# Linear attention on one core: the tiles that DMAs touch move to multiples of 2 KB in SBUF

## The chip, the cores and the metric

The kernel runs on one core of one Trainium2 chip. A core has TensorE (PE in the profile, with weight loads as PEld), VectorE (DVE), ScalarE (ACT), GpSimd (POOL) and SyncE (SP), a working memory of 128 partitions (SBUF), an accumulator memory (PSUM) and 16 DMA engines between SBUF and HBM. The metric is the device time in microseconds, less being better. The kernel before takes 126.41 us, the median of three runs (126.26 to 126.86).

## The reference

Inputs Q, K and V are float32 of 8 batches x 12 heads x 512 positions x 64 features. The attention is linear: no softmax, but a positive feature map.

```python
Q_feat = np.maximum(0, Q) + 1
K_feat = np.maximum(0, K) + 1
KV = np.einsum('bhkd,bhkv->bhdv', K_feat, V)
K_sum = np.sum(K_feat, axis=2)
numerator = np.einsum('bhqd,bhdv->bhqv', Q_feat, KV)
denominator = np.einsum('bhqd,bhd->bhq', Q_feat, K_sum)
return (numerator / (denominator[:, :, :, None] + 1e-10)).astype(np.float32)
```

In bytes: three inputs of 12.58 MB are read and one output of 12.58 MB is written.

## The kernel before

The 96 heads are taken in six steps (s = 0 to 5), each of 2 x 8 heads. A partition holds 32 consecutive positions of one head, so a step's tile `k_raw`, `v_raw` or `q_raw` is 128 partitions x 2 x 32 x 64 in bfloat16: 8 KB in each partition, 1 MB in all. The DMA that fills it reads float32 (2 MB) and casts on the way; such DMAs are issued by GpSimd (line 128), which also issues the stores of steps 0 to 4 (line 135). SyncE issues the very first K load, uncast, into a buffer of the output pool (line 121), and the three stores of the last step (line 135).

For each step, VectorE makes K features (`kf`, line 144, in two copies, each of which keeps every second head of 16 partitions) and Q features (`qf`, line 164), VectorE and ScalarE copy V blocks into `v_all` (line 156), whose zeros keep the four groups of 32 partitions apart, and TensorE accumulates K^T V and the sums of K together in `kva_ps` (line 175). ScalarE brings these into `kva` (lines 189 and 193). TensorE transposes Q features (line 199), ScalarE copies them to `qt` (line 204), TensorE multiplies them by `kva` (line 216), and VectorE takes the reciprocal of the denominators (line 232) and multiplies it in (line 233) into the output tile `o_sb`: float32, 128 partitions x 8 x 8 x 64, so 16 KB in each partition. A store takes every second of the eight rows of 2 KB of each partition, which land in HBM as rows of 2 KB.

The order of the work is written out by hand for each engine, as lists of tasks (`ORDER`); each engine works through its list in order, and semaphores follow from which tiles are read and written. GpSimd's list is its loads and stores:

```python
    POOL="""
        lv2 lk2 lq2 lv3 lq3 lk3 lk4 lv4 lq4 s00 lv5 lk5 s01 lq5 s10 s11 s20 s21 s30 s31 s40 s41
    """,
```

`lk4` is the K load of step 4, `s21` the second store of step 2. Loads of steps 0 and 1 go ahead of the list. The pools of `k_raw`, `v_raw`, `q_raw`, `kf`, `qf` and `qt` have two buffers each, so a load of step s waits for the last reader of step s - 2; the output pool has four.

A tile's SBUF address follows from the order in which the pools are opened. They are laid one behind the other from byte 16512 of each partition (8 x 2 KB + 128). The constants come first: the identity, masks, both `v_all` of 16640 bytes and both `kva` of 2080 bytes, together 37,888 bytes, so that the pools behind them begin at byte 54,400, which is 26 x 2048 + 1152. The tiles that follow are of 8 KB or 16 KB, so every tile behind the constants, those that DMAs touch among them, begins 1152 bytes beyond a multiple of 2 KB.

Of the kernel before, what the change touches and what calls it, by code (L numbers as in the profile page):

```python
# [8 lines left out]
FP32 = mybir.dt.float32  # L9
# [4 lines left out]
BANK = 512  # L14
OUT_BUFS = 4
KF_BUFS = 2
LOWEST = -3.4028234663852886e38

TASKS = dict(
# [33 lines left out]
def kernel(  # L53
# [13 lines left out]
    P = 128  # L67
# [12 lines left out]
    v_dram = view(V, ROWS)  # L80
    o_dram = view(out, C)

    const = ctx.enter_context(tc.tile_pool(name="const", bufs=1))
    k_pool = ctx.enter_context(tc.tile_pool(name="k_pool", bufs=2))
    v_pool = ctx.enter_context(tc.tile_pool(name="v_pool", bufs=2))
    q_pool = ctx.enter_context(tc.tile_pool(name="q_pool", bufs=2))
    kf_pool = ctx.enter_context(tc.tile_pool(name="kf_pool", bufs=KF_BUFS))
    qf_pool = ctx.enter_context(tc.tile_pool(name="qf_pool", bufs=2))
    mid_pool = ctx.enter_context(tc.tile_pool(name="mid", bufs=2))
    out_pool = ctx.enter_context(tc.tile_pool(name="out_pool", bufs=OUT_BUFS))  # L90
    recip_pool = ctx.enter_context(tc.tile_pool(name="recip", bufs=4))
    psum_kva = ctx.enter_context(tc.tile_pool(name="psum_kva", bufs=2, space=bass.MemoryType.PSUM))
    psum = ctx.enter_context(tc.tile_pool(name="psum", bufs=2, space=bass.MemoryType.PSUM))
    psum_qt = ctx.enter_context(tc.tile_pool(name="psum_qt", bufs=2, space=bass.MemoryType.PSUM))

    identity = const.tile([P, P], BF16, name="identity")
    ones = const.tile([P, 4], BF16, name="ones")
    zero = const.tile([P, 1], FP32, name="zero")
# [143 lines left out]
    def masks():  # L242
# [7 lines left out]
        nc.vector.tensor_scalar(  # L250
            out=shift, in0=least, scalar1=-1.0, scalar2=-LOWEST, op0=ALU.add, op1=ALU.mult
        )
# [14 lines left out]
    def needs(engine, task):  # L267
# [10 lines left out]
        if x == "kf":  # L278
            n = 2 * s + at[0] - KF_BUFS
            return [("load", s, "k"), ("kv", n // 2, n % 2, 3)]  # L280
# [136 lines left out]
```

## Time and profile before

| | us |
|---|---|
| median of three runs | 126.41 |
| the runs | 126.26 to 126.86 |
| the profiled execution | 126.19 |
| its span, first to last instruction | 124.4 |
| VectorE busy | 93.5 (75%) |
| TensorE busy | 82.0 (66%) |
| ScalarE busy | 74.3 (60%) |
| GpSimd busy | 25.1 (20%) |

The page describes one execution. The busy rows cut the span into 40 slices of 3.1 us; a digit is the busy share in tenths, and in the DMA row the mean share of the 16 DMA engines. The GB/s row counts the bytes of a packet as recorded, which for a casting load is the bfloat16 size, half of what is read from HBM. DMA queue q0 is GpSimd's, whose descriptors software writes, q1 is SyncE's, written by hardware, and q8 and q14 fetch instructions. A DMA's work is cut into packets, each on one of 16 DMA engines; at its end each engine writes 4 bytes to say that it is done. The trace records start, duration and size of each packet, and its DMA view counts them for any stretch of time. "us to landing" is from a DMA's issue to the last of these 16 notes.

### The profile page before, as it was taken

The page shows a single profiled execution, that of the slowest core. Times are in us where ns is not written, and L with a number is a line of the kernel's source. Part 1 is how long each engine was busy: PE and PEld are TensorE (multiplying, and loading weights), DVE is VectorE, ACT ScalarE, POOL GpSimd, SP SyncE. Part 2 cuts the span into 40 slices and gives each one's busy share as a digit, 9 for nine tenths or more (in the row PEclk, how much of TensorE's full clock was granted, in tenths as well). Part 3 has the DMA queues.
Part 4 walks back from the last instruction along what each step waited for, and adds up shares of the span by engine and source line. Part 5 has one row for each costly group of instructions (what it writes and reads, how often), then busy time and mean ns, then how long its engine had stood idle before and what let it go on. Part 6 is the DMA issues. An engine that isn't in the chain of part 4 may idle for free.

```text
span 124.4 us, 2353 instructions
## 1 busy us (share of the span) xinstructions
PE 82.0 (66%) x960; PEld 61.8 (50%) x960; DVE 93.5 (75%) x188; ACT 74.3 (60%) x94; POOL 25.1 (20%) x52
## 2 busy tenths in 40 slices
PE   0000099963999895879439998979598798956000
PEld 0000078842767773568326776856376686633000
DVE  4799953459589596995969799999389999699100
ACT  7538000665586999829991289955999936830000
POOL 6991042000006000063000391202200202020000
PEclk9999999998699999999986999999999999995555
DMA  3999999999999999999999999999999999999993
GB/s 84 336 215 212 217 215 216 211 211 221 211 215 217 216 207 219 213 216 213 213 213 216 215 216 291 296 215 215 288 300 238 399 417 417 410 398 398 385 387 138
DMA packets 8731, 32.13 MB, mean 258 GB/s; under 512 B 528, under 2 KB 528, under 8 KB 8592
## 3 DMA queue, kind: packets, MB, share of 16 engines
q0 software_dynamic: 7504, 28.84, 94.4%
q1 hardware_dynamic: 1216, 3.15, 6.9%
q8 instruction: 7, 0.11, 0.3%
q14 instruction: 4, 0.03, 0.1%
HBM read 37.75 MB, written 12.58 MB: 405 GB/s over the span
## 4 chain that ended last, share of the span: by engine, by line
DMA 50%; DVE 20%; ACT 8%; issue 7%; PE 5%; POOL 2%; POOLq 0%
DMA q_raw<-in_Q_dram 35%; DMA k_raw<-in_K_dram 15%; DVE o_sb L233 9%; ACT v_all L156 5%; DVE kf L144 4%; DVE qf L164 4%; ACT qt L204 2%; PE kva_ps L175 2%; DVE v_all L156 2%; DVE recip L232 2%; PE o_ps L216 2%; PE qt_ps L199 1%; ACT kva L189 1%; POOL v_raw L128 1%; POOL k_raw L128 0%
## 5 line engine op out<-in xcount | busy, mean ns | idle before, releaser
L175 PE MATMUL kva_ps<-v_all,kf 128*128 128x260 bf16 x384 | 53.4, 290 | 23.1 <-DVE v_all L156 18.0
L175 PEld LDWEIGHTS <-kf 128*128 128x128 bf16 x384 | 36.7, 102 | 32.8 <-DVE v_all L156 19.2
L156 ACT COPY v_all<-v_raw 32x2048 bf16<-32x2048 bf16 x19 | 36.0, 1896 | 7.7 <-DMA v_raw<-in_V_dram 4.1
L233 DVE TENSOR_TENSOR o_sb<-o_ps,recip 128x512 f32<-128x512 f32 x48 | 33.2, 692 | 1.7
L204 ACT COPY qt<-qt_ps 128x1024 bf16<-128x1024 bf16 x24 | 23.8, 1014 | 10.1 <-PE qt_ps L199 9.8
L216 PE MATMUL o_ps<-kva,qt 128*64 128x130 bf16 x384 | 20.9, 235 | 6.2 <-DVE o_sb L233 4.2
L144 DVE TENSOR_SCALAR kf<-k_raw,shift,least 128x2048 bf16<-128x2048 bf16 x22 | 16.9, 811 | 9.2 <-DMA k_raw<-in_K_dram 7.8
L156 DVE COPY v_all<-v_raw 32x2048 bf16<-32x2048 bf16 x29 | 20.1, 693 | 1.2 <-DMA v_raw<-in_V_dram 0.5
L216 PEld LDWEIGHTS <-qt 128*64 128x64 bf16 x384 | 13.2, 114 | 14.8 <-DVE o_sb L233 6.0
L189 ACT CAST kva<-kva_ps 64x256 bf16<-64x256 f32 x24 | 8.9, 371 | 17.1 <-PE kva_ps L175 16.7
L199 PE MATMUL qt_ps<-identity,qf 128*128 128x128 bf16 x192 | 15.0, 223 | 3.4 <-ACT qt L204 1.9
L199 PEld LDWEIGHTS <-qf 128*128 128x128 bf16 x192 | 12.3, 100 | 4.9 <-issue 2.0
L135 POOL DMA_DIRECT2D out_dram<-o_sb x10 | 8.0, 803 | 30.1 <-DVE recip L232 18.7
L128 POOL DMA_DIRECT2D v_raw<-in_V_dram x7 | 4.8, 683 | 39.6 <-DVE recip L232 17.9
L164 DVE TENSOR_SCALAR qf<-q_raw 128x1024 bf16<-128x1024 bf16 x24 | 8.8, 429 | 5.2 <-DMA q_raw<-in_Q_dram 5.2
L232 DVE RECIPROCAL recip<-o_ps 128x8 f32<-128x8 f32 x48 | 9.6, 200 | 2.4 <-PE o_ps L216 2.1
L128 POOL DMA_DIRECT2D k_raw<-in_K_dram x6 | 4.2, 697 | 13.3 <-DVE kf L144 13.3
L128 POOL DMA_DIRECT2D q_raw<-in_Q_dram x6 | 5.1, 842 | 1.2 <-DVE qf L164 1.2
L258 DVE MEMSET v_all<- 128x2600 f32 x2 | 4.5, 2225 | 1.1 <-issue 1.1
L193 ACT CAST kva<-kva_ps 64x4 bf16<-64x4 f32 x24 | 4.1, 171 | 0.0
L259 ACT COPY v_all<-zero 128x1560 f32<-128x1560 f32 x2 | 2.9, 1488 | 0.0
L144 DVE TENSOR_SCALAR kf<-o_sb,shift,least 128x2048 bf16<-128x2048 f32 x2 | 2.6, 1340 | 0.0
(18 smaller groups left out, 6.6 us busy)
## 6 DMA issues: line engine op xcount, KB each, us to landing
out_dram<-o_sb POOLq DMA_DIRECT2D x10, 1024.0 KB, 22.4
q_raw<-in_Q_dram POOLq DMA_DIRECT2D x6, 1024.0 KB, 23.8
k_raw<-in_K_dram POOLq DMA_DIRECT2D x5, 1024.0 KB, 19.3
v_raw<-in_V_dram POOLq DMA_DIRECT2D x5, 1024.0 KB, 18.3
o_sb<-in_K_dram SPq DMA_DIRECT2D x1, 1024.0 KB, 4.9
v_raw<-in_V_dram POOLq DMA_DIRECT2D x2, 512.0 KB, 8.6
out_dram<-o_sb SPq DMA_DIRECT2D x1, 1024.0 KB, 8.7
out_dram<-o_sb SPq DMA_DIRECT2D x2, 512.0 KB, 7.7
```

Source lines behind the costliest of these rows:

```text
L128: nc.gpsimd.dma_start(out=t[:, ns[0] : ns[-1] + 1], in_=drams[x][:, 2 * s + ns[0] : 2 * s + ns[-1] + 1])
L135: engine.dma_start(out=o_dram[:, 8 * s : 8 * s + 8][:, ms], in_=outs[s][:, ms], single_packet=engine is nc.gpsimd,)
L144: nc.vector.tensor_scalar(out=kf[:, :, a], in0=raw["k", s, n], scalar1=shift[:, a : a + 1], scalar2=least[:, a : a + 1], op0=ALU.add, op1= ...
L156: copy(out=v_alls[n][ps, :, b * D : b * D + D], in_=raw["v", s, n][ps])
L164: nc.vector.tensor_scalar(out=qf[:, :, cs, n], in0=rows[:, :, cs], scalar1=1.0, scalar2=1.0, op0=ALU.add, op1=ALU.max,)
L175: nc.tensor.matmul(kva_pss[s, n], lhsT=kfs[s, n][:, c].rearrange("p a d -> p (a d)"), rhs=v_alls[n][:, c], start=(c == 0), stop=(c == ROWS ...
L189: nc.scalar.copy(out=kva[po, a::2, n, 0:D], in_=kva_ps[pi, 0 : 4 * D].rearrange("p (b d) -> p b d", b=4),)
L199: nc.tensor.transpose(qt_ps[:, c, r], qfs[s][:, r, 2 * i + c], identity)
L204: copy(out=qts[s][:, 2 * i : 2 * i + 2], in_=qt_pss.pop((s, i)).rearrange("p c r q -> p c q r"),)
L216: nc.tensor.matmul(o_ps[64 * t : 64 * t + 64, c // 2, (c % 2) * W : (c % 2) * W + W], lhsT=qts[s][:, 4 * i + c, 16 * k : 16 * k + 16], rhs ...
L232: nc.vector.reciprocal(out=recip, in_=cells[:, :, :, :, D:D1])
L233: nc.vector.tensor_tensor(out=outs[s][:, e + 2 * u :: 4, 4 * i : 4 * i + 4].rearrange("p n (b c) d -> p b c n d", b=2), in0=cells[:, :, :, ...
```

## The change

A pool `head` with one tile of 480 float32 (1920 bytes in each partition) that nothing reads or writes is opened first. It fills the 1920 bytes from 16512 to 18432, which is 9 x 2048. Behind it come the pools of the tiles that DMAs read or write (`k_raw`, `v_raw`, `q_raw`, then the output tiles), then `kf`, `qf`, `qt` and the reciprocals, and last the constants. All tiles of 8 and 16 KB now begin at multiples of 2 KB. The constants' addresses have the same remainders by 2 KB as before. Each engine's instructions, their order and their waits are the same; they carry other addresses.

```diff
+HEAD = 480
...
-    const = ctx.enter_context(tc.tile_pool(name="const", bufs=1))
+    head = ctx.enter_context(tc.tile_pool(name="head", bufs=1))
     k_pool = ctx.enter_context(tc.tile_pool(name="k_pool", bufs=2))
     v_pool = ctx.enter_context(tc.tile_pool(name="v_pool", bufs=2))
     q_pool = ctx.enter_context(tc.tile_pool(name="q_pool", bufs=2))
+    out_pool = ctx.enter_context(tc.tile_pool(name="out_pool", bufs=OUT_BUFS))
     kf_pool = ctx.enter_context(tc.tile_pool(name="kf_pool", bufs=KF_BUFS))
     qf_pool = ctx.enter_context(tc.tile_pool(name="qf_pool", bufs=2))
     mid_pool = ctx.enter_context(tc.tile_pool(name="mid", bufs=2))
-    out_pool = ctx.enter_context(tc.tile_pool(name="out_pool", bufs=OUT_BUFS))
     recip_pool = ctx.enter_context(tc.tile_pool(name="recip", bufs=4))
+    const = ctx.enter_context(tc.tile_pool(name="const", bufs=1))
...
+    head.tile([P, HEAD], FP32, name="spacer")
```

## The prediction

> **What bounds the kernel now.** I read the page first: its rows by slices, the DMA queues, the chain of waits.
>
> ```profile
> span 124.4 us, 2353 instructions
> ...
> DVE  4799953459589596995969799999389999699100
> ...
> DMA  3999999999999999999999999999999999999993
> GB/s 84 336 215 212 217 215 216 211 211 221 211 215 217 216 207 219 213 216 213 213 213 216 215 216 291 296 215 215 288 300 238 399 417 417 410 398 398 385 387 138
> ...
> q0 software_dynamic: 7504, 28.84, 94.4%
> q1 hardware_dynamic: 1216, 3.15, 6.9%
> ...
> DMA 50%; DVE 20%; ACT 8%; issue 7%; PE 5%; POOL 2%; POOLq 0%
> ```
>
> The DMA row is 9 from the second slice to the last but one, and the two data queues together hold 101% of the 16 DMA engines (packets of one engine overlap a little). No compute engine is as full: VectorE has 75% in the page. The chain gives DMA only half, because it steps back from an issue to the compute that released it; whether that compute mattered depends on whether the DMA queue was empty when the issue came. So next, when POOL's issues went out and when they landed: two lines of POOL's timeline, then the issue lines of the DMA view for 53 to 54.5 us and for 109 to 116:
>
> ```profile
> 53.87 0.71 POOL L128 DMA_DIRECT2D k_raw<-in_K_dram  x1 [13.25 <-DVE kf L144]
> ...
> 108.93 0.75 POOL L135 DMA_DIRECT2D out_dram<-o_sb  x1 [3.90 <-DVE recip L232]
> ```
>
> ```profile
> k_raw<-in_K_dram POOLq DMA_DIRECT2D x1, 1024.0 KB, 14.1
> ```
>
> ```profile
> out_dram<-o_sb POOLq DMA_DIRECT2D x1, 1024.0 KB, 9.9
> out_dram<-o_sb SPq DMA_DIRECT2D x1, 1024.0 KB, 8.7
> out_dram<-o_sb SPq DMA_DIRECT2D x2, 512.0 KB, 7.7
> ```
>
> The last number is us from issue to landing. A load's own transfer is 4.9 us (below) and a store's 2.5, so the K load that waited longest for compute still stood some 9 us behind other transfers, the last POOL store 7.4 us, and the two halves on SP about 5 (7.7 less 2.7 for both). The DMA engines never run dry: compute could be some 5 us late anywhere without being seen, and a faster compute engine buys nothing. The kernel's time is the sum of its DMA packets, so I need the price of one packet of each kind. The DMA view of four stretches, 20 to 70 us (loads alone), 98 to 108 (POOL's stores), 109 to 116 (the same, later), 118.6 to 121.6 (SP's stores):
>
> ```profile
> DMA packets 2767, 10.72 MB, mean 214 GB/s; under 512 B 160, under 2 KB 160, under 8 KB 2762
> ...
> q0 software_dynamic: 2762, 10.66, 105.9%
> q8 instruction: 3, 0.05, 0.4%
> q14 instruction: 2, 0.02, 0.1%
> ```
>
> ```profile
> DMA packets 1075, 4.16 MB, mean 416 GB/s; under 512 B 64, under 2 KB 64, under 8 KB 1073
> ...
> q0 software_dynamic: 1073, 4.13, 101.7%
> ```
>
> ```profile
> DMA packets 713, 2.78 MB, mean 397 GB/s; under 512 B 38, under 2 KB 38, under 8 KB 711
> ```
>
> ```profile
> DMA packets 596, 1.16 MB, mean 386 GB/s; under 512 B 30, under 2 KB 30, under 8 KB 596
> ```
>
> Packets under 512 B are the 4-byte completion writes. Loads: (2762 - 160)/16 = 162.6 packets per DMA engine in 50 us, 307.5 ns each, 306 without the 0.5% for instruction fetches. The packet records give it sharper: on the engine that finishes first the completions of whole loads (16 packets per engine) follow at 4.895 us and of half loads (8) at 2.461, so a load packet, 8192 B read and 4096 B written, takes 304.2 ns and a completion 27. POOL's stores: 1009/16 = 63.1 per engine in 10 us, 158.6 ns; on the engine that finishes first whole stores follow at 2.49 us, so (2490 - 27)/16 = 153.9 ns for a packet of 4096 B, two rows of 2 KB. Late POOL stores: 673/16 = 42.1 in 7 us, 166.4. SP's stores, packets of one row of 2 KB: 566/16 = 35.4 in 3 us, 84.8.
>
> These make up the span: the first K load ends at 5.1; 17.5 loads x 4.895 = 85.7; 10 POOL stores x 2.49 = 24.9; 64 SP packets x 84.8 ns = 5.4; sum 121.1. The last packet ends at 123.2. The 2.1 left are instruction fetches of up to 1.1 us on single engines and the slower late stores. The profiled execution's own time is 126.19, 1.8 beyond its span and 0.2 under the median of the three runs, 126.41.
>
> **The change part by part.** It adds a spacer tile that nothing touches, and reorders pools. Engine streams, waits and DMA shapes are the same instruction for instruction; only SBUF addresses differ. Nothing is moved past a queue and no wait is added.
>
> *Compute operands.* kf, qf, qt, recip, v_all and kva lie elsewhere. kf keeps its distance to k_raw in these remainders, qf to q_raw; v_all and kva keep their remainder to 2 KB. No row shows any price for the address of an operand; the bounds are zero and whatever the 5 us of slack swallows, so zero either way. If the cover were gone, the chain's DVE pieces (0.69 us per norm) would be what is late next.
>
> *Load packets*, 280 per DMA engine. Their SBUF side starts 128 B past a multiple of 256 (1152 = 4 x 256 + 128), afterwards on one. They move 4096 B into SBUF but read 8192 from HBM, and whatever the write has extra lies under the read. From above: per byte the load packet (304.2/8192 = 37.1 ps) is cheaper than the store packet (37.6), so no row shows a faster one. A line through both kinds has 2 x 153.9 - 304.2 = 3.6 ns per packet that does not go with bytes; if all of that were alignment, 280 x 3.6 = 1.0 us goes. Taken: zero, since it is the same 3.6 for one row as for two.
>
> *POOL store packets*, 160 per engine: they read two rows of 2 KB from SBUF, each now starting halfway between multiples of 256. Were half a 256 B piece read for nothing at each row, 128 B at 26.9 B/ns = 4.75 ns, a packet would carry 9.5 ns. But it stands only 153.9 - 152.1 = 1.8 above half a load packet, so there is no room for it. Bounds 0 and 160 x 3.6 = 0.6 us gained; taken zero.
>
> [...]
>
> *SP store packets*, 64 per engine: 84.8 ns against 3.6 + 2048 x 0.0367 = 78.8 by the line, 6.0 more. That would fit one half piece (4.75). But the first K load's 8192 B packets on SP's queue are recorded at 309 ns, and the instruction fetches of 8192 B during the run, which do not touch the kernel's tiles, at 309 to 322. So packets issued by hardware look dearer whatever they touch. Bounds: 64 x 6.0 = 0.38 us gained, or nothing; taken nothing.
>
> *A loss.* All DMA tiles sat at one remainder before, so the trace shows no other. The nearest row of a dearer packet is the late stretch, 166.4 less 158.6, 7.8 ns above the same packets earlier. Bounds 0 and, for the some 115 POOL store packets per engine before 109 us, 115 x 7.8 = 0.9 us; taken zero.
>
> Sum: 126.19 + 0 for the profiled execution; between that and the median of the runs I say 126.3.
>
> **The rivals.**
>
> *Boundaries cost after all (faster).* Half a piece on each SBUF row read goes: 160 x 9.5 + 64 x 4.75 = 1.8 us, giving 124.5. For it: the SP packets carry about one such piece. Against: the POOL packets. In part, it can be the SP packets (0.38) and the late stores' 7.8 ns on 45 packets (0.35): 0.73, giving 125.6. Chance of a gain over 0.63 us from here: 0.23.
>
> *Rows at multiples of 2 KB make SBUF accesses collide (slower).* The place is the packet's SBUF side; the cause of the late stretch's dearer packets would reach all stores: +0.9, giving 127.2. It decides from 0.63 us, that is 5.5 ns on each of those 115, or 2.3 on each load packet. For it: that stretch shows that the same packet can get dearer with the loads gone. Against: within a DMA engine all rows stood at one remainder before too, and stores at 98 to 108 us show nothing of it. Chance 0.14.
>
> *The change does not do what it says.* The spacer could be dropped as unused. It is not: the first K tile goes from byte 54400 to 18432, which is 9 x 2048. Chance 0.01, and the time would be 126.3 too.
>
> **How the numbers follow.** No measurable change 0.62 and the idle spacer 0.01; faster 0.23; slower 0.14. A measurement of this kernel tells 0.5%, 0.63 us, from no change. The forecast is 126.3, its own range 125.7 to 126.9. The range of all reaches to 124.8, leaving out the whole boundary gain (0.08), and to 127.2, leaving out loads that collide as well (0.06).
>
> **What would show it.** Right: loads alone again some 163 packets per DMA engine in 50 us, POOL stores 63 in 10 us, SP stores 35 in 3 us, and a full DMA row. The boundary rival shows 67 POOL stores in 10 us and SP packets near 79 ns; the collision shows fewer than 61, or loads under 160. I am wrong if the packets' price moves at all; wrong about the cover if the DMA row gets a gap and packets keep their price.

## The result and the profile after

The changed kernel takes 125.77 us (median of 20 runs, 125.47 to 126.67), the kernel before 126.44 in its 20 runs beside it: the ratio is 0.9952 with a 95% interval of 0.9937 to 0.9966, a gain of 0.61 us (the medians stand 0.67 apart). The forecast was 126.3, with a range of 125.7 to 126.9: no change that a measurement can tell, the limit being put at 0.5%. The measured 0.48% is inside that limit, but the interval excludes no change: the change does something, and the forecast said that it does nothing.

The profiled execution took 125.95 us with a span of 124.2. Its page:

```profile
span 124.2 us, 2353 instructions
...
DVE  4799963459589696995979799999389999799200
...
DMA  3999999999999999999999999999999999999992
GB/s 95 333 214 214 215 212 212 215 214 216 214 215 214 212 214 215 215 215 215 215 212 214 215 215 277 310 199 214 277 318 227 389 414 417 416 414 416 408 406 107
...
q0 software_dynamic: 7504, 28.84, 94.5%
q1 hardware_dynamic: 1216, 3.15, 6.7%
```

The DMA row is full as before, and in the GB/s row the slices of loads are what they were (some 215). The difference stands in the last eight slices: before they fell from 417 to 410, 398, 398, 385 and 387, now they hold 414 to 417 and then 408 and 406. The DMA view of 20 to 70 us, loads alone, has the same number of packets as before to the last one:

```profile
DMA packets 2767, 10.72 MB, mean 214 GB/s; under 512 B 160, under 2 KB 160, under 8 KB 2762
```

Now the two stretches where they part, in the DMA view of the kernel before, 109 to 115 us (POOL's late stores) and 118.6 to 121 (SP's):

```profile
DMA packets 614, 2.39 MB, mean 398 GB/s; under 512 B 35, under 2 KB 35, under 8 KB 612
...
q0 software_dynamic: 612, 2.36, 101.1%
```

```profile
DMA packets 477, 0.93 MB, mean 387 GB/s; under 512 B 23, under 2 KB 23, under 8 KB 477
```

The same two of the kernel after:

```profile
DMA packets 645, 2.48 MB, mean 414 GB/s; under 512 B 40, under 2 KB 40, under 8 KB 644
...
q0 software_dynamic: 644, 2.47, 101.9%
```

```profile
DMA packets 502, 0.98 MB, mean 408 GB/s; under 512 B 24, under 2 KB 24, under 8 KB 502
```

Packets under 512 B are completion notes, recorded at 4 bytes each, and come off. POOL's late stores: (612 - 35)/16 = 36.1 packets per DMA engine in 6 us before, 166.4 ns each; (644 - 40)/16 = 37.8 after, 158.9 ns. That is 7.5 ns on each of the 48 packets that a DMA engine has left from 109 us on, 0.36 us. SP's stores: (477 - 23)/16 = 28.4 in 2.4 us before, 84.6 ns; 29.9 after, 80.3 ns. That is 4.3 ns on each of 64 packets, 0.27 us. The sum, an estimate of 0.63 us, accounts for the measured gain. The two profiled executions themselves end only 0.24 us apart. Averaged over the 16 engines, the completions show why: at 109 us the kernel after stands 0.15 us behind, then gains 0.31 us on POOL's late stores and 0.31 on SP's, and on average an engine finishes 0.47 us earlier.

The packet records say more than the means. All 1024 SP store packets of after are recorded at 84 ns; before, 346 of them were at 84, the others mostly at 86, 88, 91 or 93. Of the POOL store packets from 109 to 115 us most are at 159 or 160 in both kernels, but before a growing part stood at 164 or more: 28% of them from 109.5 to 114 us, and half from 114 to 115. So the price of a quick packet has not changed. What has gone are most of the packets that took longer now and then: 4% stand at 164 ns or more in after from 109 to 115 us, 31% in before. From 98 to 105 us, before shows as little of it as after, 5% in each.

### The profile page after: what moved, and what is told of

Same layout as the page of the kernel before. It is cut to its first block, busy times and chain, and to the rows that moved or that the text cites. A ratio compares the mean times of both kernels' runs of the same rounds, so it can differ in the third digit from the quotient of the medians.

```text
span 124.2 us, 2353 instructions
## 1 busy us (share of the span) xinstructions
PE 82.6 (67%) x960; PEld 62.0 (50%) x960; DVE 93.5 (75%) x188; ACT 74.3 (60%) x94; POOL 25.2 (20%) x52
## 4 chain that ended last, share of the span: by engine, by line
DMA 39%; DVE 20%; PE 13%; ACT 12%; POOL 6%; issue 2%; POOLq 0%; ACTq 0%
DMA q_raw<-in_Q_dram 20%; DMA k_raw<-in_K_dram 18%; DVE o_sb L236 9%; ACT v_all L159 8%; PE kva_ps L178 7%; DVE kf L147 4%; PE o_ps L219 3%; DVE v_all L159 3%; ACT qt L207 3%; DVE recip L235 2%; DVE qf L167 2%; POOL kva L383 2%; PE qt_ps L202 2%; POOL v_raw L131 2%; POOL q_raw L131 1%
## 5 line engine op out<-in xcount | busy, mean ns | idle before, releaser
L178 PE MATMUL kva_ps<-v_all,kf 128*128 128x260 bf16 x384 | 54.6, 294 | 22.6 <-DVE v_all L159 17.6
L178 PEld LDWEIGHTS <-kf 128*128 128x128 bf16 x384 | 37.4, 104 | 33.2 <-DVE v_all L159 18.2
```

Of the source, the lines that this page charges most:

```text
L178: nc.tensor.matmul(kva_pss[s, n], lhsT=kfs[s, n][:, c].rearrange("p a d -> p (a d)"), rhs=v_alls[n][:, c], start=(c == 0), stop=(c == ROWS ...
```

## The experiments

**Which tiles, and does the place matter?** The theory formed from the two traces: the stores' rows in SBUF begin off a boundary, and that is what lets late store packets be held up. Rivals: the gain comes from the loads' destinations, or from the new order of the pools rather than the remainder.

`out_2k` puts the load tiles back:

```diff
-HEAD = 480
+HEAD = 768
...
+    gap = ctx.enter_context(tc.tile_pool(name="gap", bufs=1))
     out_pool = ctx.enter_context(tc.tile_pool(name="out_pool", bufs=OUT_BUFS))
...
+    gap.tile([P, 224], FP32, name="gap_spacer")
```

> All as after the change, but k_raw, v_raw and q_raw begin 1152 bytes past a multiple of 2 KB, as before; the output tiles are at multiples. Theory (the gain is in the stores' reads from SBUF): ratio to before 0.995, SP packets all at 84 ns. Loads rival (the gain is in the loads' writes): ratio 1.000.

`loads_2k` puts the output tiles back (a gap of 288 float32 ahead of them, one of 224 behind):

> All as after the change, but the output tiles begin 1152 bytes past a multiple of 2 KB, as before; the load tiles are at multiples. Theory: ratio to before 1.000, SP packets spread over 84 to 93 ns. Loads rival: 0.995.

`order_1152` keeps the new order of the pools and puts every tile of 8 and 16 KB back to 1152:

```diff
-HEAD = 480
+HEAD = 768
...
+    gap = ctx.enter_context(tc.tile_pool(name="gap", bufs=1))
     const = ctx.enter_context(tc.tile_pool(name="const", bufs=1))
...
+    gap.tile([P, 224], FP32, name="gap_spacer")
```

> The pools in the order of after, but a longer spacer puts all tiles of 8 and 16 KB 1152 bytes past a multiple of 2 KB, as before. Theory (the remainder matters, the place does not): ratio to before 1.000, SP packets spread. Place rival (the gain is from the order of the pools): 0.995.

`mult_256` is the kernel before with 128 bytes between the constants and the rest:

```diff
+    pad = ctx.enter_context(tc.tile_pool(name="pad", bufs=1))
     k_pool = ctx.enter_context(tc.tile_pool(name="k_pool", bufs=2))
...
+    pad.tile([P, 32], FP32, name="spacer")
```

> The kernel before with a spacer of 128 bytes behind the constants: all DMA tiles begin 1280 bytes past a multiple of 2 KB, which is a multiple of 256 but not of 512. Theory with a boundary of 256: ratio to before 0.995, SP packets all at 84 ns. With a boundary of 512 or 2 KB: 1.000 and the spread.

Measured, with the mean record of a late POOL store packet (109 to 115 us; the few records of 250 ns and more are left out) and of an SP store packet, each from one profiled execution:

| kernel | ratio to before (95%) | late POOL, ns | SP, ns |
|---|---|---|---|
| before | 1 | 165.1 | 87.0 |
| after | 0.9952 (0.9937 to 0.9966) | 160.4 | 84.0 |
| out_2k | 0.9951 (0.9934 to 0.9968) | 160.3 | 84.0 |
| loads_2k | 1.0008 (0.9989 to 1.0027) | 166.0 | 86.8 |
| order_1152 | 1.0008 (0.9993 to 1.0023) | 165.9 | 87.0 |
| mult_256 | 0.9967 (0.9949 to 0.9984) | 160.5 | 84.0 |

The DMA view from 109 to 115 us has it too, here `loads_2k`:

```profile
DMA packets 610, 2.36 MB, mean 393 GB/s; under 512 B 35, under 2 KB 35, under 8 KB 609
```

and `mult_256`:

```profile
DMA packets 637, 2.46 MB, mean 410 GB/s; under 512 B 37, under 2 KB 37, under 8 KB 636
```

The four split cleanly. The output tiles carry the whole gain, the load tiles and the order of the pools nothing, and a multiple of 256 that is none of 512 gives the same packets as multiples of 2 KB. Both rivals fall.

**The price by itself, first try.** Two kernels that only store. These and the other kernels of bare stores below ran once each. In both, one tile begins at a multiple of 2 KB and another off it, and three stores of each take turns:

```python
for engine in (nc.sync, nc.gpsimd):
    for i in range(12):
        src = (at_r, at_0)[i // 3 % 2]
        s, e = i // 2, i % 2
        engine.dma_start(
            out=o_dram[:, 8 * s : 8 * s + 8][:, e::2],
            in_=src[:, e::2],
            single_packet=engine is nc.gpsimd,
        )
```

> This kernel leaves out all loads and all computation: it stores two constant tiles over the whole output, first in 12 stores of 1 MB by SP, then again in 12 by POOL. In each dozen three stores come from a tile at 1152 bytes past a multiple of 2 KB, then three from a tile at a multiple, and so again. Theory (where the SBUF row starts makes a store packet dearer from time to time): SP packets of 2 KB are spread over 84 to 93 ns in the 1152 blocks and all at 84 in the others; POOL packets of 4 KB are at 159 or 160 with a share of 171 to 175 in the 1152 blocks, and without it in the others; the 1152 blocks take some 3% longer. Boundary rival (every row pays a half piece): the 1152 blocks are dearer by 5 ns on every SP packet and 9.5 on every POOL packet. Chance rival (the spread comes from elsewhere, such as HBM at that moment): both kinds of block look alike.

> As the kernel with 1152, without loads and computation, but the second tile begins 64 bytes past a multiple of 2 KB. Theory: a start off a multiple of 256 is enough, so the blocks from this tile show the same spread as those at 1152 (which is 128 past a multiple of 256). Rival (only multiples of 128 or of 64 matter, or none): no spread at 64, the blocks alike.

These two were laid out badly: each POOL store waited only for the SP store of its own rows, so from 17 us on both queues ran side by side, mostly from different tiles, and packets of both kinds of tile were spread. Only the first stretch tells something. There SP stores alone, from the tile off the boundary, and the DMA view from 12 to 17 us is the same line in both kernels, at 1152 and at 64 bytes:

```profile
DMA packets 943, 1.87 MB, mean 373 GB/s; under 512 B 32, under 2 KB 32, under 8 KB 943
```

(943 - 32)/16 = 56.9 packets per DMA engine in 5 us, 87.8 ns. So for SP's stores 64 bytes past a multiple of 256 is as dear as 128.

**The queues apart.** POOL's dozen first, then SP's in the opposite order of rows, so that SP's first store waits for POOL's last:

```diff
-        for engine in (nc.sync, nc.gpsimd):
+        for engine in (nc.gpsimd, nc.sync):
...
+                j = i if engine is nc.gpsimd else 11 - i
-                s, e = i // 2, i % 2
+                s, e = j // 2, j % 2
```

> Stores of two constant tiles alone, as in the first kernel of that kind, without loads and computation, but the two queues do not mix: first 12 stores of 1 MB by POOL, then 12 by SP, each dozen as three from the tile at 1152, three from the one at a multiple of 2 KB, and so again (the second dozen writes in the opposite order, so its first waits for POOL's last). The slope theory (off a multiple of 256 a store packet is dearer whenever stores run alone): POOL's 1152 blocks have a share of packets at 166 to 178 from their first store on and take over 2.55 us a store, its others 2.49; SP's 1152 blocks take 2.8 us a store, its others 2.70. The onset theory (it takes some us of pure stores, as the kernel before was free of it until about 107 us): POOL's first block is clean, its second is not.

The DMA view of this kernel, first POOL from the tile at 1152 (30 to 35 us), then from the one at 0 (37 to 41), then SP from 1152 (47 to 52) and from 0 (56 to 61):

```profile
DMA packets 484, 1.88 MB, mean 376 GB/s; under 512 B 25, under 2 KB 25, under 8 KB 484
```

```profile
DMA packets 433, 1.67 MB, mean 418 GB/s; under 512 B 25, under 2 KB 25, under 8 KB 433
```

```profile
DMA packets 947, 1.87 MB, mean 375 GB/s; under 512 B 32, under 2 KB 32, under 8 KB 947
```

```profile
DMA packets 1026, 2.04 MB, mean 407 GB/s; under 512 B 32, under 2 KB 32, under 8 KB 1026
```

By the records of completions, averaged over the DMA engines, POOL's stores at 1152 follow each other at 2.76 to 3.00 us, those at 0 at 2.58 to 2.60 right behind slow ones and at 2.49 to 2.50 in the second such block; SP's at 2.75 to 2.81 and 2.57, but for one: the first from 1152 behind SP's quick block still took 2.57, and the two after it 2.75 and 2.77. In packets per DMA engine, 28.7 in 5 us against 25.5 in 4 for POOL, that is 174 and 157 ns; for SP 57.2 against 62.1 in 5 us, 87.4 and 80.5 ns. So off the boundary, with nothing else running, a POOL packet costs 17 ns more than in the second block at 0, and an SP packet 7. POOL had no onset, its first stores were the slowest. The kernel before does otherwise: its stores stayed quick from 98 to 105 us.

**Why were they quick there?** Two things stood around those stores that the bare kernel lacked, loads just before and busy engines beside:

```python
for i in range(6):
    nc.gpsimd.dma_start(out=raws[i], in_=k_dram[:, 2 * i : 2 * i + 2])
for j in range(6):
    store(j)
nc.vector.memset(at_r[:, 0:2], 2.0)
nc.vector.tensor_copy(out=x[:, 0:64], in_=at_r[:, 0, 0])
for j in range(6, 12):
    store(j)
for k in range(22):
    nc.vector.tensor_copy(out=y, in_=x)
...
```

> All of the reference's computation is left out. POOL issues six loads of 1 MB (2 MB read), then six stores from a constant tile at 1152 bytes past a multiple of 2 KB, then, behind a rewrite of that tile, six more of them, beside which VectorE copies for about 15 us, ScalarE copies and TensorE multiplies. It asks why the kernel before has its store packets at 159 ns until about 107 us, though its rows start off a multiple of 256 throughout. If recent loads keep such stores quick, the first stores behind the loads follow at 2.49 us and later ones of the first six at 2.75 or more, the second six all at 2.75. If busy engines keep them quick, the second six follow at 2.49 as long as the engines are busy. If neither, all twelve follow at 2.75.

The DMA view from 35 to 40 us (behind the loads) and from 56 to 61 (behind the pause, beside busy engines):

```profile
DMA packets 544, 2.10 MB, mean 419 GB/s; under 512 B 32, under 2 KB 32, under 8 KB 544
```

```profile
DMA packets 462, 1.82 MB, mean 365 GB/s; under 512 B 17, under 2 KB 17, under 8 KB 462
```

All six stores behind the loads are quick, to the end, at 2.49 to 2.51 us, packets at 159 or 160, though every row starts 128 bytes off: (544 - 32)/16 = 32 packets in 5 us, 156 ns. After a pause of 3.7 us without a data packet the same stores from the same tile take 2.69 to 3.00, with all engines busy (27.8 packets, 180 ns). Busy engines did not keep these stores quick (180 ns); right behind loads they were (156 ns). Whether it is the loads or the missing pause, this kernel does not separate. None of the forecasts was quite this: the first said that the effect of the loads would wear off within six stores.

**Either side, or both?** The last kernel moves the HBM rows as well, by 128 bytes. Four blocks of three stores, SP in the order A to D, then POOL from D to A:

```python
blocks = [(at_0, hbm_128, 0, 0), (at_128, hbm_128, 0, 3), (at_0, hbm_0, 1, 0), (at_128, hbm_0, 1, 3)]
```

> Stores of two constant tiles alone; all loads and computation are left out, and half of the output is written 128 bytes beside its place. Four blocks of three stores of 1 MB, first by SP, then in the opposite order by POOL. Block A: SBUF rows on multiples of 2 KB, HBM rows 128 bytes past a multiple of 256; B: both 128 past; C: both on multiples; D: SBUF rows 128 past, HBM rows on multiples (as the kernel before has it). If the SBUF side's start alone counts, A and C are quick (2.57 us a store by SP, 2.49 by POOL) and B and D slow (2.75 to 2.81; 2.7 or more). If what counts is how far the two sides stand apart, A and D are slow and B and C quick. If any side off a multiple of 256 counts, only C is quick.

| us between completions | A | B | C | D |
|---|---|---|---|---|
| SP, A to D | 2.79 to 2.80 | 2.79 to 2.80 | 2.61, 2.57, 2.57 | 2.57 |
| POOL, D to A | 2.64, 2.75, 2.75 | 2.77, 2.83, 2.75 | 2.62, 2.58, 2.59 | 2.96, 2.81 |

SP's blocks A and B (12 to 17 us in the DMA view), then D (33 to 38):

```profile
DMA packets 934, 1.88 MB, mean 376 GB/s; under 512 B 16, under 2 KB 16, under 8 KB 934
```

```profile
DMA packets 1024, 2.05 MB, mean 409 GB/s; under 512 B 25, under 2 KB 25, under 8 KB 1024
```

An HBM side 128 bytes off a multiple of 256 made stores dear, even with SBUF on one (A, 2.79 to 2.80 us on SP against 2.57 to 2.61 in C), and equal offsets on both sides did not help (B, 2.79 to 2.80 too), so the relative distance is out. The packets of A's first store are still recorded at 84 ns, and only the later ones at about 92. Block C is quick on SP. On POOL it takes 2.58 to 2.62 us behind D, better than the other blocks but not the 2.49 that was expected. Block D is the surprise: rows like those that were slow in the bare kernels go at full speed behind C on SP, every packet at 84 ns, and are the slowest of all on POOL, where they come first.

**Better than both?** Two variants of after, in which POOL issues the last step's first store, or all three. These stores move from SP's list of tasks to the end of POOL's; the line that picks the engine, for the first variant:

```diff
-            store(s, stores_of(s)[at[0]][0], nc.sync if s == last else nc.gpsimd)
+            store(s, stores_of(s)[at[0]][0], nc.sync if s == last and at[0] else nc.gpsimd)
```

> After the change, with the first store of the last step (1 MB) issued by POOL behind its others in place of SP. Its 32 packets of 2 KB per DMA engine at 84 ns become 16 of 4 KB at 154, so 0.22 us less: ratio to before 0.993 to 0.994 where after has 0.995. If the DMA engines gain nothing by it (POOL's issue comes too late, or the queue has run dry), 0.995.

> After the change, with all three stores of the last step issued by POOL. By the packets alone 64 x 84 ns become 32 x 154, 0.45 us less: ratio 0.992. If the last one is held up by POOL's longer way from issue to first packet, with the queue ahead of it empty, that is lost again: 0.995 or above.

`s50_pool` has 125.72 us and a ratio of 0.9936 (0.9912 to 0.9960): in the expected place, but its interval holds after's 0.9952 too, so whether it is better is not settled. `s5_pool` is slower than before, 126.85 and 1.0033 (1.0017 to 1.0049), though its packets save what they should: the last ends at 122.5 us, against 122.9 in after. The loss lies behind it. SP's waits in after, then in `s5_pool`:

```profile
SPq L415 <- PEq L415: 0.6, 2, 0.5
```

```profile
SPq L412 <- PEq L412: 1.8, 2, 1.3
```

The span ends 2.5 us behind the last packet in place of 1.3, in a wait of the closing barrier at the last line. Expected was a loss on POOL's way from issue to first packet, and that was not where it was.

## Why the prediction was right or wrong

The bound was read rightly. The DMA row stayed full, loads kept their packets to the last one, and the gain is the sum of dearer packets removed. That compute does not matter fits `order_1152`, where every tile moves and the time stays (1.0008). The term for load packets (zero) was right, by `loads_2k` (1.0008).

Two terms were mis-sized. *SP store packets*, "0.38 us gained, or nothing; taken nothing": about 0.27 was gained. The reason for taking nothing, that packets issued by hardware look dearer whatever they touch, explained a part that did not move: the quick SP packet is recorded at 84 ns before and after. The means of that stretch held a second part, the spread above 84, and only the whole distribution shows it. The reason was also weaker than it looked, since it set recorded durations (309 ns) beside the spacing of load packets (304.2): the load packets themselves are recorded at 324. *POOL store packets*, "Bounds 0 and 160 x 3.6 = 0.6 us gained; taken zero": about 0.36 was gained. The argument, 1.8 ns over half a load packet leaves no room for a half piece per row, was taken from quick stores on the engine that finishes first. The prediction had read the late stretch, 7.8 ns dearer, but its sum used it only as the price of a possible loss. It was the cost that the change removes, in plain sight.

That the time still fell inside the range, 0.07 us from its edge, is luck: the mechanism of the forecast was no change at all. By its own sign, "I am wrong if the packets' price moves at all", it was wrong. Its signs of being right could not show that. The kernel after has 163 load packets from 20 to 70 us, (1075 - 64)/16 = 63 POOL stores from 98 to 108 us and (598 - 34)/16 = 35 SP stores from 118.6 to 121.6 us, all as forecast. Its DMA view, from 98 to 108 us and from 118.6 to 121.6:

```profile
DMA packets 1078, 4.18 MB, mean 418 GB/s; under 512 B 64, under 2 KB 64, under 8 KB 1075
...
q0 software_dynamic: 1075, 4.14, 101.7%
```

```profile
DMA packets 598, 1.16 MB, mean 385 GB/s; under 512 B 34, under 2 KB 34, under 8 KB 598
...
q1 hardware_dynamic: 598, 1.16, 99.3%
```

But the first stretch of stores lies almost wholly ahead of the dearer packets, and in the second the engines of the kernel after were already finishing, the first at 121.2 us.

So the boundary rival came true in its partial form: it gave "the SP packets (0.38) and the late stores' 7.8 ns on 45 packets (0.35): 0.73, giving 125.6", and about 0.27 and 0.36 were measured. Its full form, a half piece on every row, is refuted by the kernel before itself and by `stores_after`: rows off the boundary ran at full speed there, at 159 or 160 ns a packet. The collision rival did not occur.

The runs fit a boundary of 256 bytes: `mult_256` has the quick packets 256 bytes off a multiple of 512 (160.5 and 84.0 ns in the table), while 64 and 128 bytes past a multiple of 256 were dear (87.8 ns for an SP packet in `stores_64` and `stores_1152`). A constant cost does not fit: measured was nothing in the first six stores of `stores_after` (156 ns a packet of two rows, against 157 on the boundary in `stores_apart`) and 17 ns per packet of two rows in `stores_apart` (174 against 157). The prediction's "so there is no room for it" held for one stretch.

What stays open is the mechanism. Shown is that stores off a multiple of 256 had two paces: 2.49 to 2.51 and 2.69 to 3.00 us a store on POOL (`stores_after`), 2.57 and 2.75 to 2.81 on SP (`stores_apart`). They kept the quick one behind loads (six stores) or for a while behind quick stores (three in block D on SP, one in `stores_apart`). POOL's were slow behind every pause (from the first on in `stores_apart`, 2.76 to 3.00 us, behind the pause of `stores_after`, 2.69 to 3.00, and in block D, 2.96 and 2.81). In the kernel before they fall from the one into the other after about 107 us: 5% of the packets are at 164 ns or more from 98 to 107 us, 14% from 107 to 109 and 31% from 109 to 115. Stores on the boundary came back to the quick pace by themselves on SP, within one store (2.61, then 2.57 us in block C, and 2.57 in `stores_apart`). POOL's did not always: behind slow stores they took 2.58 to 2.62 us for all three stores of block C and of the first block at 0 in `stores_apart`, and only its second such block was at 2.49 to 2.50 at once.

What knocks the kernel before out of the quick pace was not tried. One rival stands in the trace: instruction fetches of 8 and 16 KB (q8 and q14) run among its stores, at 98.1, 102.2, 109.1 and 113.4 us, and none among the stores of `stores_after`, which stayed quick. The share of packets at 164 ns or more jumps behind the last fetch, from some 30% to 50% and more, but its first rise, at 107 us, comes ahead of the fetch at 109.1.

## What to carry to other kernels

Try the rows that DMAs store at multiples of 256 bytes on both sides; it costs a spacer, and on the SBUF side here it gave 0.5% (0.9951 in `out_2k`) of a kernel that is bound by DMA all along. The HBM side was tried in bare stores alone, where 128 bytes off took 2.79 to 2.80 us a store on SP and a multiple 2.57 to 2.61. The stores were the place to look here: the tiles of loads that cast, and read twice what they write, changed nothing (1.0008 in `loads_2k`). A price taken from the best stretch of a trace is a lower bound. Where the same packets get dearer later, ask which of the two is the normal state, and read the distribution before calling the difference a fixed cost. Choose signs for the stretch in which a rival would show, not for the one that was read first.

## What the runs showed of the hardware

The same store, from the same tile to the same kind of rows, took 2.49 to 2.51 us right behind loads and 2.69 to 3.00 behind a pause, when its rows began off a multiple of 256 bytes (`stores_after`; on SP 64 or 128 bytes past made no difference, 87.8 ns a packet at both). On the boundary SP's stores took 2.57 us from the second one on (`stores_apart`, block C of `stores_hbm`); POOL's took 2.58 to 2.62 in two blocks of three and 2.49 to 2.50 in a third, all behind slow stores. The quick packets were mostly recorded at 159 or 160 ns (two rows, POOL) and 84 (one row, SP), in whole kernels and bare stores alike. And finishing with a POOL store put 1.2 us more between the last packet and the end than finishing with SP's (2.5 against 1.3), in one profiled execution each.
